# A gated unit at the DMA limit: all loads and stores on one queue, in the order store i, load i+2

## Chip, cores, metric

One core of one Trainium2 chip. The metric is device time in microseconds (us), the median of several executions. The experiments were spread over five chips; each was timed beside the kernel before, whose median lay between 933.28 and 933.66 us on all of them.

## The reference

```python
x = randn(8192, 8192) as float32          # 268 MB read
a, b = np.split(x, 2, axis=-1)
return a * (1 / (1 + np.exp(-b)))         # 8192 x 4096 float32, 134 MB written
```

## The kernel before

The input is cut into 32 tiles of 256 rows. A tile is 128 partitions by 64 KB (two rows side by side, each `a | b`), its output 128 partitions by 32 KB. There are two input slots and two output slots. ScalarE takes the sigmoid of `b` in place, VectorE multiplies. Loads are issued by the sync sequencer, stores by the scalar sequencer. Tiles 0 and 31 are worked in four chunks; tile 31 is also stored in four.

```python
R = 2; SLOTS = 2
x_t = x.rearrange("(n p r) m -> n p (r m)", p=P, r=R)
out_t = out.rearrange("(n p r) m -> n p (r m)", p=P, r=R)
xs = [pool.tile([P, R * n_cols], fp32, ...) for k in range(SLOTS)]
os = [pool.tile([P, R * half], fp32, ...) for k in range(SLOTS)]
...
for i in range(n_tiles):
    load = nc.sync.dma_start(out=xs[i % SLOTS], in_=x_t[i])     # waits for multiply i-2
    ...
    def store(cols):
        ins = nc.scalar.dma_start(out=out_t[i, :, cols], in_=os[i % SLOTS][:, cols])
    for k, (r, c) in enumerate(parts):      # one part; four in tiles 0 and 31
        sig = nc.scalar.activation(out=b, in_=b, func=SIG)
        mul = nc.vector.tensor_mul(out=packed[:, r, c], in0=rows[:, r, 0, c], in1=b)
        ...   # `implied(...)` drops waits that follow from others; in odd tiles
        ...   # the sigmoid, not the multiply, waits for the output slot
        if i == n_tiles - 1 and k > 0:
            store(chunks[k - 1])
    store(chunks[-1] if i == n_tiles - 1 else slice(0, R * half))
```

## Time and profile before

| | before |
|---|---|
| time | 933.28 us (933.08 to 933.77, 3 runs) |
| span of the profiled run | 931.7 us |
| bytes | 402.67 MB, 432 GB/s over the span |
| ScalarE, VectorE busy | 24%, 30% |
| DMA busy | 90% or more in each of 40 slices |

The table says that the 16 DMA engines never rest, so the kernel stands at the transfer limit; its lines are shown in the prediction. Beside the profile's views I use the trace's packet records: the start, length, size and queue of each packet that a DMA engine moved. Joining each packet to the one that starts where it ends gives 16 chains, one for each engine. The list of packets that one queue has on one engine is called its ring below.

### The profile page before, as it was taken

How to read it: one execution, taken by the hardware profiler on the slowest of the kernel's cores; microseconds unless marked ns; L12 is line 12 of the kernel's file. 1: busy time of each engine (PE TensorE's matmuls, PEld its weight loads, DVE VectorE, ACT ScalarE, POOL GpSimd, SP SyncE). 2: the span in 40 equal slices, each digit the busy share in tenths (PEclk: the TensorE clock that was granted, in tenths of full speed). 3: DMA queues.
4: the chain of work that ended last, by engine and by line, in shares of the span. 5: the costliest groups of instructions: out<-in, count | busy, mean ns of one | idle time of the engine just before them, and what ended most of it. 6: DMA issues, size and time to landing. Idle time of an engine off the chain costs nothing.

```text
span 931.7 us, 247 instructions
## 1 busy us (share of the span) xinstructions
DVE 278.7 (30%) x38; ACT 227.1 (24%) x39; POOL 0.2 (0%) x4
## 2 busy tenths in 40 slices
DVE  0333213333133331233312333123331233312333
ACT  1323330233311333113331133311333113332033
POOL 0000000000000000000000000000000000000000
DMA  9999999999999999999999999999999999999999
GB/s 405 428 450 428 422 456 405 450 428 428 450 418 438 428 436 442 428 428 450 447 408 428 442 459 428 413 460 411 450 428 425 453 408 447 428 428 450 425 430 405
DMA packets 9649, 402.67 MB, mean 432 GB/s; under 512 B 1072, under 2 KB 1072, under 8 KB 1072
## 3 DMA queue, kind: packets, MB, share of 16 engines
q1 hardware_dynamic: 4608, 268.44, 66.6%
q10 hardware_dynamic: 5040, 134.22, 33.4%
q14 instruction: 1, 0.01, 0.0%
HBM read 268.44 MB, written 134.22 MB: 432 GB/s over the span
## 4 chain that ended last, share of the span: by engine, by line
DMA 73%; DVE 15%; ACT 12%; issue 0%; ACTq 0%
DMA x_sb<-in_x_dram 73%; DVE o_sb L69 15%; ACT x_sb L68 12%; ACTq L62 0%; ACTq L68 0%
## 5 line engine op out<-in xcount | busy, mean ns | idle before, releaser
L69 DVE TENSOR_TENSOR o_sb<-x_sb 128x8192 f32<-128x8192 f32 (+1 forms) x38 | 278.7, 7344 | 647.1 <-ACT x_sb L68 647.1
L68 ACT ACTIVATE x_sb<-x_sb 128x8192 f32<-128x8192 f32 (+1 forms) x38 | 225.8, 5952 | 695.6 <-DMA x_sb<-in_x_dram 694.4
L68 ACT ACT_TABLE_LOAD x1 | 1.3, 1283 | 0.8 <-PEq L188 0.8
L188 POOL MEMSET const-bfloat16-1.0<- 128x1 bf16 x1 | 0.1, 102 | 0.0
L188 POOL MEMSET const-uint8-127<- 128x1 uint8 x1 | 0.1, 102 | 0.0
L188 POOL MEMSET const-float32-0.0<- 128x1 f32 x1 | 0.1, 99 | 0.2 <-issue 0.2
L188 POOL MEMSET const-float32-1.0<- 128x1 f32 x1 | 0.1, 99 | 0.0
## 6 DMA issues: line engine op xcount, KB each, us to landing
out_dram<-o_sb ACTq DMA_DIRECT2D x31, 4096.0 KB, 34.7
out_dram<-o_sb ACTq DMA_DIRECT2D x4, 1024.0 KB, 5.6
x_sb<-in_x_dram SPq DMA_DIRECT2D x32, 42.2
```

The costliest lines, as they stand in the source:

```text
L68: sig = nc.scalar.activation(out=b, in_=b, func=SIG)
L69: mul = nc.vector.tensor_mul(out=packed[:, r, c], in0=rows[:, r, 0, c], in1=b)
L188: nc = _bacc.Bacc("TRN2", target_bir_lowering=False, num_devices=1)
```

## The change

The intent: loads and stores share one first-in-first-out queue, so that each load runs at the full rate, each store follows in its turn, and the scalar sequencer is left to compute. The final tile's small stores stay on the scalar queue, so that they need not stand behind the last whole store.

```diff
+    def load(i, queue):
+        ins = queue(out=xs[i % SLOTS], in_=x_t[i])
+        ...
+    for i in range(SLOTS):
+        load(i, nc.sync.dma_start)
     for i in range(n_tiles):
-        load = nc.sync.dma_start(out=xs[i % SLOTS], in_=x_t[i])
         ...
-            by_sigmoid = i % 2 == 1 and len(parts) == 1
-            implied(mul, *(s for s in old["stores"] if by_sigmoid or s not in freed))
-            if by_sigmoid: ...                  # slot's wait on the sigmoid
+            implied(mul, *(s for s in old["stores"] if s not in freed))
             if i == n_tiles - 1 and k > 0:
-                store(chunks[k - 1])
-        store(chunks[-1] if i == n_tiles - 1 else slice(0, R * half))
+                store(chunks[k - 1], nc.scalar.dma_start)
+        if i == n_tiles - 1:
+            store(chunks[-1], nc.scalar.dma_start)
+        else:
+            store(slice(0, R * half), nc.sync.dma_start)
+        if i + SLOTS < n_tiles:
+            load(i + SLOTS, nc.sync.dma_start)
```

More of the change, by code (lines that the diff above doesn't have):

```diff
@@ L42, in _tiles @@
     last_stores = [[] for _ in range(SLOTS)]
+    loads = []
+    def load(i, queue):
+        old = gone[i % SLOTS]
+        ins = queue(out=xs[i % SLOTS], in_=x_t[i])
+        implied(ins, *old["loads"], *old["sigs"])
+        loads.append(ins)
+    for i in range(SLOTS):
+        load(i, nc.sync.dma_start)
     for i in range(n_tiles):
@@ L46, in _tiles @@
         now = {k: [] for k in old}
+        now["loads"].append(loads[i])
         rows = xs[i % SLOTS].rearrange("p (r h m) -> p r h m", r=R, h=2)
         packed = os[i % SLOTS].rearrange("p (r m) -> p r m", r=R)
-        load = nc.sync.dma_start(out=xs[i % SLOTS], in_=x_t[i])
-        implied(load, *old["loads"], *old["sigs"])
-        now["loads"].append(load)
         if 0 < i < n_tiles - 1:
@@ L60, in _tiles, with store @@
             ]
-        def store(cols):
-            ins = nc.scalar.dma_start(out=out_t[i, :, cols], in_=os[i % SLOTS][:, cols])
+        def store(cols, queue):
+            ins = queue(out=out_t[i, :, cols], in_=os[i % SLOTS][:, cols])
             now["stores"].append(ins)
@@ L71, in _tiles @@
             implied(mul, *old["muls"], *old["loads"], *now["loads"])
-            by_sigmoid = i % 2 == 1 and len(parts) == 1
-            implied(mul, *(s for s in old["stores"] if by_sigmoid or s not in freed))
-            if by_sigmoid:
-                for s in freed:
-                    tc.add_manual_dep(sig.ins, s.ins.name, DEP, reason="frees the output slot")
+            implied(mul, *(s for s in old["stores"] if s not in freed))
             tc.keep_in_program_order(sig)
```

## The prediction

> **What bounds the kernel now.** I read the page's engine shares first, then its DMA lines, then a table of stretches, then the waits and the timeline. The page, with the row of busy tenths for DMA in 40 slices:
>
> ```profile
> span 931.7 us, 247 instructions
> DVE 278.7 (30%) x38; ACT 227.1 (24%) x39; POOL 0.2 (0%) x4
> ...
> DMA  9999999999999999999999999999999999999999
> ...
> q1 hardware_dynamic: 4608, 268.44, 66.6%
> q10 hardware_dynamic: 5040, 134.22, 33.4%
> ...
> HBM read 268.44 MB, written 134.22 MB: 432 GB/s over the span
> ```
>
> The two compute engines are idle 70% and more; DMA is at 90% or above in every slice. Queue q1 (loads, sync) and q10 (stores, scalar) together fill 66.6 + 33.4 = 100% of 16 engines' span, in the ratio of their bytes (2 to 1). Is there a hole hidden in the rounding? The table of stretches (start:end, length, busy DVE, ACT, POOL, PE clock, DMA share, GB/s) says no for the body:
>
> ```profile
> 60.58:118.66 58.08, 17.39 (x2) 14.06 (x2) 0.00 (x0) 1.00 1.00 433
> 118.66:873.00 754.34, 226.00 (x26) 182.81 (x26) 0.00 (x0) 1.00 1.00 434
> ```
>
> DMA share 1.00 over two tiles and over 26 tiles. The trace's own packet records go further. Packets start in rounds of 16 (one per DMA engine), and each round starts when the previous ends. A round of load packets (64 KB each) lasts 2.415 us, so a load (8 rounds) takes 19.32 us; a round of store packets (32 KB) lasts 1.211 us, a 4 MB store 9.69 us; a final 1 MB store, eight rounds of 8 KB packets at 0.308 us, takes 2.47 us. Sum: 32 x 19.32 + 31 x 9.69 + 4 x 2.47 = 928.5 us. Add 1.0 us before the first packet and 1.55 us by which 32 early load packets run longer than their usual 2.418 us (start of the kernel, and 36 us, at the first store): 931.1 us. The last packet ends at 931.37. So all but 0.3 us of the run is packets back to back, and the bound is **bytes through 16 DMA engines**. The chain of waits (73% load, 15% multiply, 12% sigmoid) is misleading here: it follows the slot loop, whose "load" share includes 19 us in which that load stands behind others.
>
> **What the waits say about the slot loop.** Waits (total us, times, longest), then issues (count, KB, us to landing):
>
> ```profile
> ACT x_sb L68 <- DMA x_sb<-in_x_dram: 694.4, 32, 22.3
> SPq L50 <- DVE o_sb L69: 859.9, 30, 31.7
> out_dram<-o_sb ACTq DMA_DIRECT2D x31, 4096.0 KB, 34.7
> out_dram<-o_sb ACTq DMA_DIRECT2D x4, 1024.0 KB, 5.6
> x_sb<-in_x_dram SPq DMA_DIRECT2D x32, 42.2
> ```
>
> The sync sequencer does nothing but wait for the multiply of tile i, then issues load i+2. That load lands 42.2 us later although its data needs 19.3 us: it queues behind load i+1 and shares with stores. A store needs 9.7 us and lands in 34.7, because it shares with loads.
>
> **What the Trainium skill says.** "DMA: Bandwidth & Descriptors", section "Queues, rings and completion order": each DMA engine takes turns between the queue rows it has work for, a packet at a time, and consumes one row's descriptors in ring order. The trace agrees with the turns: after 40 us the rounds alternate, one of loads, one of stores. Same page, section "Issuing engines are not separate DMA queues": all issuers' transfers "run on the same 16 DMA engines and interleave", and a second issuer saves only sequencer time. The trace agrees: the two queues' shares add up to 100%, and the issue that moves costs 0.36 us. Same page, "Where 436 GB/s comes from": a ceiling of 435.2 GB/s for a core; the body here runs at 434, so by this too nothing is left in the rate.
>
> **The change, part by part.**
>
> *Stores move to the sync queue.* 31 issues of 0.36 us leave the scalar sequencer (11 us in total, where ACT waits 694 us for loads: worth nothing) and join the sync sequencer, which waits 860 us of 932. Store i and load i+2 wait for the same multiply, so neither holds back the other; the load is issued about 0.35 us later than now.
>
> *Sharing becomes first in, first out.* The ring order becomes L0 L1 S0 L2 S1 L3 ... The bytes and packet sizes are the same, so the work stays 928.5 us; the question is only whether the ring ever runs dry. Follow tile i, whose load lands at t. Sigmoid 7.03 us, multiply 8.69 us and handoffs take it to t + 15.8: then S(i) and L(i+2) are issued. At about t - 1.6 (in the first load, the last packet ends at 21.58 at the latest and ACT starts at 21.95; at the last, 913.1 and 914.7; I take the longer) the ring turned to S(i-1) and L(i+1), 29.0 us of work, so it runs dry at t + 27.4. The new work arrives **11.6 us** before that. The first two loads fill the ring to 1.0 + 0.7 + 2 x 19.32 = 40.3, and the first multiply is over at
>
> ```profile
> 21.95 7.31 ACT L68 ACTIVATE x_sb<-x_sb 128x2048 f32<-128x2048 f32 x4 [19.89 <-DMA x_sb<-in_x_dram]
> 23.89 8.90 DVE L69 TENSOR_TENSOR o_sb<-x_sb 128x2048 f32<-128x2048 f32 x4 [23.89 <-ACT x_sb L68]
> 32.82 0.38 ACTq L62 DMA_DIRECT2D out_dram<-o_sb  x1
> ```
>
> 32.82 us, 7.5 us early. Landing times follow: a store 11.6 + 9.7 + 1.6 = 23 us (now 34.7), a load 11.6 + 9.7 + 19.3 + 1.6 = 42.2 us (as now). Output slots are free long before they are wanted, so taking the slot's wait from sigmoid to multiply costs nothing. Effect on the end: 0.
>
> *The tail.* Now S30 shares with L31, and L31's data is in at 913.1. In the new order S30 stands behind L31, so L31 is in one store's part earlier: 931.4 - (9.69 + 4 x 2.47) = 911.8, landing at 913.4. The scalar queue's stores came 4.3, 6.5, 8.9 and 11.1 us after the landing in the old tail:
>
> ```profile
> 914.71 3.71 ACT L68 ACTIVATE x_sb<-x_sb 128x2048 f32<-128x2048 f32 x2 [21.75 <-DMA x_sb<-in_x_dram]
> ...
> 918.98 0.34 ACTq L62 DMA_DIRECT2D out_dram<-o_sb  x1
> 921.18 0.34 ACTq L62 DMA_DIRECT2D out_dram<-o_sb  x1
> 923.63 2.54 ACTq L62 DMA_DIRECT2D out_dram<-o_sb  x2
> ```
>
> So issues at about 917.7, 919.9, 922.3, 924.5. S30 keeps the engines busy until 921.5 alone; the four small stores need 2.47 us each after it, starting at the latest at 921.5, 924.0, 926.4, 928.9. Each is issued about 4 us ahead, and the only doubt is how soon its packets follow. The tail should stay filled: 0, perhaps +2 us (below).
>
> Sum: 0 + 0 + 0 to 2; expected 0.1. From 933.28, **933.4 us**.
>
> **Rivals.**
>
> 1. *A bubble where a load follows a store in one ring.* Now the other queue could cover such a bubble. Against: load 0 to load 1 is a boundary inside one ring with the other empty, and the rounds start at 16.18, 18.59, 21.01, 23.42: no bubble at 21.01. The final stores also follow each other in one ring at 0.308 us a round without a step. No boundary between a store and a load in one ring can be seen before. 62 such boundaries at 0.05 us would make 936.4; slower by over 2% needs 18.7 us, 0.30 us each, about an eighth of a load packet. I give 3%.
>
> 2. *The scalar queue's first use.* The first store of all was issued at 32.82 and its first packets started at 38.81, 6 us later, with one load round stretched by 0.87 us. That queue's first use now falls in the tail. With 6 us of delay the first small store would start at 923.7 instead of 921.5: +2.2 us, 935.5. For it: it was seen. Against: in those 6 us two 2.4 us load rounds were already under way; behind 1.21 us store rounds the wait is shorter.
>
> 3. *A gain, from fewer turns between reads and writes or a shorter tail.* Loads alone (1 to 35 us) run at 2.415 us a round and stores alone (914 to 921) at 1.211, the same as mixed, so turns cost nothing to be saved; and no idle time is left to fill. At best the stretched first packets go: -1.5 us, 931.8. Faster by 2% would need over 450 GB/s. 1%.
>
> **Range and chances.** Down: 1.5 us of start-up plus a little noise (three runs span 0.7 us). Up: rival 2, or a small rival 1. Range 931.8 to 936.4; faster 0.01, same 0.96, slower 0.03.
>
> **What would show it right or wrong.** Right: DMA share 1.00 at 434 GB/s in the body, q1 holding nearly all bytes, stores landing in 23 us, loads in 42 us, sync still mostly waiting for multiplies, the second load landing near 42 us (now 44.8). Rival 1: share under 1.00 in the body and load rounds that step by more than 2.415 us at a change of direction. Rival 2: a hole around 921 to 924 us only. Wrong altogether: loads landing later than 43 us with ACT waiting over 22 us a tile, which would mean a cost of a single ring that no row here shows.

## The result

The changed kernel took **938.15 us** (936.89 to 940.78, 4 runs) against 933.24 (933.08 to 933.77, 4 runs). The ratio is **1.0055**, 95% interval 1.004 to 1.007. A ratio is the mean time of one kernel's runs over that of the other's of the same rounds, so not quite the ratio of the medians. Executions over 1.5% slower than the fastest of the same kernel are left out of the means. The loss is clear of noise, and the time lies above the predicted range of 931.8 to 936.4.

The page of the changed kernel:

```profile
span 935.5 us, 235 instructions
DVE 278.8 (30%) x38; ACT 227.0 (24%) x39; POOL 0.2 (0%) x4
...
DMA  9999999999999999999999999999999999999998
...
q1 hardware_dynamic: 9072, 398.46, 98.7%
q10 hardware_dynamic: 576, 4.19, 1.1%
```

Nearly all bytes are now on q1. The DMA row looks full; only the last slice shows something, 8 for 9. The stretches over two tiles and 26 tiles (columns as in the prediction: DMA share and GB/s last):

```profile
58.58:116.98 58.40, 17.38 (x2) 14.06 (x2) 0.00 (x0) 1.00 1.01 434
116.98:874.19 757.21, 226.01 (x26) 182.76 (x26) 0.00 (x0) 1.00 1.00 433
```

The same two tiles took 58.08 us before and take 58.40 now, the same 26 tiles 754.34 and 757.21: most of the 3.8 us of span is lost in the body, at a DMA share of 1.00. The waits and issues:

```profile
ACT x_sb L76 <- DMA x_sb<-in_x_dram: 695.8, 32, 22.6
SPq L70 <- DVE o_sb L77: 874.3, 31, 31.6
out_dram<-o_sb SPq DMA_DIRECT2D x31, 4096.0 KB, 22.9
x_sb<-in_x_dram SPq DMA_DIRECT2D x32, 41.8
```

A store lands 22.9 us after its issue (23 predicted), a load 41.8 (42.2 predicted). So the queue works as worked out. The tail, on the timeline:

```profile
916.02 3.71 ACT L76 ACTIVATE x_sb<-x_sb 128x2048 f32<-128x2048 f32 x2 [21.95 <-DMA x_sb<-in_x_dram]
...
920.29 0.38 ACTq L70 DMA_DIRECT2D out_dram<-o_sb  x1
922.49 0.91 ACTq L70 DMA_DIRECT2D out_dram<-o_sb  x1
```

The last load was to land at 913.4; the sigmoid that waits for it starts at 916.02, 2.6 us later. Where do these come from, if the engines were never idle?

**The packet records show it.** An engine's packet of load is 2.418 us long in the rule. The last load packet ahead of a store is longer than that ("stretched") on 1 to 16 engines, by 0.05 to 0.6 us (up to 1.1 in a second record, taken later), and what an engine loses so it keeps: it runs behind the others from then on. How far the slowest is behind the fastest is called the lag. When each engine came to its first packet of the store of tile k:

```
                   fastest engine (us)         slowest engine behind it (us)
store of tile      0      7      16     30      0     4     7     12    16    30
changed kernel   41.35  244.74 505.76 911.76   0.76  1.16  2.45  3.13  3.90  3.90
a second record  41.41  244.6  505.6  911.6    0.62  3.21  3.96  5.04  5.64  5.72
before: the 16 semaphore writes that close a load lie 0.6 us apart, in every tile
```

The fastest engine keeps 29.00 us a tile and reaches the last store at 911.76; the prediction had 911.8. The slowest, 3.90 us behind, still has that store (9.69 us) and four small ones (9.88 us) before it: 911.76 + 3.90 + 9.69 + 9.88 = 935.2. The last packet of the record ends at 935.15. The second record gives 936.9 by the same sum, and ends at 936.8. So the loss in these records is **the lag of the slowest of 16 engines**. A transfer is not done until its slowest engine is (the last packet of load 31 ends at 915.66, and its sigmoid starts at 916.02), while the busy share, a mean over engines that are all busy, shows none of this.

### The profile page after: what moved, and what is told of

Its sections match the earlier page's. It is cut to its first block, busy times and chain, and to the rows that moved or that the text cites. A ratio compares the mean times of both kernels' runs of the same rounds, so it can differ in the third digit from the quotient of the medians.

```text
span 935.5 us, 235 instructions
## 1 busy us (share of the span) xinstructions
DVE 278.8 (30%) x38; ACT 227.0 (24%) x39; POOL 0.2 (0%) x4
## 2 busy tenths in 40 slices
DMA packets 9650, 402.67 MB, mean 430 GB/s; under 512 B 1072, under 2 KB 1072, under 8 KB 1072
## 4 chain that ended last, share of the span: by engine, by line
DMA 72%; DVE 15%; ACT 12%; SPq 1%; issue 0%; ACTq 0%
DMA x_sb<-in_x_dram 72%; DVE o_sb L77 15%; ACT x_sb L76 12%; SPq L70 1%; ACTq L70 0%
## 6 DMA issues: line engine op xcount, KB each, us to landing
out_dram<-o_sb SPq DMA_DIRECT2D x31, 4096.0 KB, 22.9
x_sb<-in_x_dram SPq DMA_DIRECT2D x32, 41.8
```

## The experiments

Three rivals at the start: the change of direction inside one ring (A), the moved wait and later issue (B), the first use of the scalar queue in the tail (D). That the first record was a one-off (C) is met by a second one. A loss of 0.5% counts as seen because its interval lies above 1. Each kernel has one packet record, but the changed kernel two.

### The changed kernel once more

No edit.

> The changed kernel unaltered, for a second packet record. In the first one the fastest DMA engine kept exactly 29.00 us a tile, but other engines had their last load packet ahead of a store stretched, by 0.05 to 0.6 us, at tiles 0 to 16 and hardly later, and fell up to 3.9 us behind the fastest. Theory A (a change from load to store inside one ring costs the engines that already lag): the same picture, some engines 3 to 5 us behind at the end, time 936.5 to 941. Theory C (a one-off of that run): lag under 1 us, time under 935.

938.47 us, ratio 1.0049 (1.0034 to 1.0064). Lag 5.7 us; load packets stretched after the first store by 21 us in all, summed over engines (25 in the first record), and hardly after tile 17. The picture repeats; which engines lag and by how much differs, and with it the time.

### Stores back on the scalar queue

```diff
-            store(slice(0, R * half), nc.sync.dma_start)
+            store(slice(0, R * half), nc.scalar.dma_start)
```

> The changed kernel with the 31 whole stores back on the scalar queue; the new program order and the wait moved from sigmoid to multiply stay. Theory A: the single ring is the cause, so 933.2 us, engines within 1 us of each other at the end. Rival B (the moved wait or the later load issue costs something): 936 to 938 us.

933.34 us, ratio 0.9995 (0.9978 to 1.0012); lag 1.3 us. All else of the change stays in this kernel, so B is refuted: the 5 us come from putting the stores on the loads' queue. Nor is it the step from a load packet to a store packet as such: with two rings each engine takes it for every one of its 248 store packets, and after the first store the load packets of this run are stretched by only 1.0 us in all, summed over engines.

### Final stores on sync as well

```diff
-                store(chunks[k - 1], nc.scalar.dma_start)
+                store(chunks[k - 1], nc.sync.dma_start)
...
-            store(chunks[-1], nc.scalar.dma_start)
+            store(chunks[-1], nc.sync.dma_start)
```

(The closing code then takes the last store of the sync queue.)

> The changed kernel with the final tile's four stores on the sync queue too. In its record eight engines had the first small packet of the scalar queue stretched by 0.8 to 1.1 us at 921.6, but those were not the engines that ended last. Theory A (lag of the slow engines sets the end): 937 to 938.5, at most 1 us less than the changed kernel. Rival D (the first use of the scalar queue in the tail costs the time): 934 or less.

938.65 us, ratio 1.0051: no gain, so D is refuted. Lag 4.5 us; the sum of above gives 911.45 + 4.52 + 19.57 = 935.5, and the last packet ends at 935.5.

### Loads on scalar, stores on sync

```diff
-            load(i + SLOTS, nc.sync.dma_start)
+            load(i + SLOTS, nc.scalar.dma_start)
```

> The changed kernel with loads 2 to 31 on the scalar queue and the stores left on sync: two rings again, with the queues' roles exchanged. If mixing directions in one ring is the cause, 933 to 933.8 us and a lag under 1.5 us. If stores on the sync queue are the cause, 938.

933.51 us, ratio 0.9999; lag about 1 us. Which queue carries what does not matter, as long as they are two. This run has a lesson in reading waits. Stores now take 49.2 us to land, and the multiply waits for them:

```profile
ACT x_sb L76 <- DMA x_sb<-in_x_dram: 690.2, 32, 22.6
DVE o_sb L77 <- DMA out_dram<-o_sb: 374.6, 19, 20.3
```

A new wait of 374.6 us in all costs nothing, because the DMA engines always have other work queued.

### Load i+2 ahead of store i

```diff
-            store(slice(0, R * half), nc.sync.dma_start)
-        if i + SLOTS < n_tiles: load(i + SLOTS, nc.sync.dma_start)
+            if i + SLOTS < n_tiles: load(i + SLOTS, nc.sync.dma_start)
+            store(slice(0, R * half), nc.sync.dma_start)
```

> The changed kernel with load i+2 issued ahead of store i: still one ring and 31 changes from load to store, but each store is in the ring about 31 us before its turn instead of 12. If the stretching is a matter of late descriptors: gone, 933.5. If it is the change of direction in one ring: as the changed kernel, 937 to 940, lag 3.5 to 6 us.

938.89 us, ratio 1.0059; lag 4.9 us. The stores stand in the ring long before their turn, and the loss is the same. It is not a matter of issuing late.

### Halves: twice the changes, or twice the transfers

Three kernels cut each load and each store in two by row. In the first, the ring order is store, load, store, load; in the second, store, store, load, load; in the third, stores are on scalar.

```diff
-            store(slice(0, R * half), nc.sync.dma_start)
+            for h in range(2):
+                store(slice(h * half, (h + 1) * half), nc.sync.dma_start)   # third: nc.scalar
+                load(i + SLOTS, nc.sync.dma_start, (h,))                    # first kernel only
```

First:

> Loads and stores of the changed kernel cut into halves by row, in ring order store, load, store, load: twice the changes from load to store in one ring, packets of half the size. Packets of half the size alone cost perhaps 0.5% (an 8 KB packet takes 0.309 us, a quarter of a 32 KB one 0.303), so about 4 us. Theory A with a fixed cost for each change: the lag of the slowest engine doubles, to 7 us, time 945. Theory A with a lag that ends by itself once engines are some us apart: lag about 4 us again, time 941.

Second:

> Halves again, but in ring order store, store, load, load: 31 changes from load to store as in the changed kernel, twice the transfers, packets of half the size. In the three whole-size records the stretching of load packets ended at tile 17, in the store-load-store-load run at tile 9, both after 17 to 18 changes and some 36 transfers. If what counts is changes of direction (or the lag they have built up): stretched packets only at the change to a store, until about tile 17, lag 3.5 to 5 us, time 939 to 941. If what counts is transfers in the ring: they end at about tile 9.

Third:

> The same halves with the stores on the scalar queue: prices the smaller packets alone. From the store-load-store-load run, whose packets add up to 3.5 us more for an engine on average than the changed kernel's: 935.5 to 937, lag under 1.5 us.

Measured: 939.05, 940.4 and 936.29 us; lag 3.5, 4.6 and 1.2 us. The third prices smaller packets at 2.7 us (ratio 1.0029). Against it, one ring costs 2.8 and 4.1 us. (The first had been forecast at 941 or 945; the smaller packets had been taken for 4 us.) In the first, stretching died out after tile 9, some 18 changes, with the lag at 3.3; in the second it faded about tile 17, after 17 changes but twice the transfers. By these two records it is changes from load to store that count, not transfers; and doubling them does not double the loss. The lag grows over some 17 changes and then stands, here and in the records of the changed kernel.

### Engines put out of step on purpose

```diff
+    for q in (0, 32):      # 8 partitions each: carried out by half of the engines
+        nc.sync.dma_start(out=os[1][q : q + 32 : 4, :], in_=x_t[1][q : q + 32 : 4, : R * half])
```

Once with one ring, once with stores on scalar.

> The changed kernel with two dummy loads of 8 partitions by 32 KB behind load 1, which only half of the engines carry out: these start 2.4 us behind the rest before the first store. If the lag limits itself (engines stretch packets while they cross from load to store together), the stretching after the first store falls well below the 16 to 25 us, summed over engines, of the three records, and the time is about 938 to 940 with a lag no larger than before. If it adds to whatever lag there is: lag 6.5 to 8 us, time 940.5 to 942.

> The two dummy loads of the skewed kernel with the stores on the scalar queue. Half the engines start 2.4 us behind. If the lag alone were what costs (engines out of step), 940 or more; if it costs only together with one ring for both directions: 933.3 plus the 2.4 us of the dummy loads, 935.5 to 936.5, and no stretched packets beyond the first store.

One ring: 944.66 us, ratio 1.0119. Two rings: 936.0 us, 1.0029. The second is as expected: lag stands at 4.5 us, and two rings are not hurt by it. The first missed both of its forecasts. The lag ended at 4.6 us, no larger than before; but now all engines, leading ones too, had packets stretched by about 1 us at some changes (such as those near 127, 215, 303, 420, 567 and 829 us) and by almost nothing at others: 119 us after the first store, summed over engines, against 25 and 21 before. My theory that being apart protects engines fell with this run: with two groups a packet apart, packets were stretched more, not less.

### Pauses in the stores, in two rings

In one ring an engine runs no store while it runs a load, so writing pauses, for 18.6 us at most and 15.4 in late tiles of the first record. Is the pause the cause, rather than the ring? Loads in halves give load and store packets one size, 32 KB; taking turns, a whole store is then done before the next comes.

```diff
-        ins = queue(out=xs[i % SLOTS], in_=x_t[i])
+        for h in range(2):
+            ins = queue(out=xs[i % SLOTS][:, cols_h], in_=x_t[i][:, cols_h])
...                                     # whole stores, on nc.scalar.dma_start
```

> Two rings with pauses in the writing: loads in halves (32 KB packets) on sync, whole stores (32 KB packets) on scalar. Taking turns packet by packet, a store now needs 19.4 us of each 29.0 us tile, so every tile has some 9.7 us without a store and then starts storing anew, as in one ring, but in another ring. If the start of storing after a pause is what stretches the loads in flight: stretched packets at many tiles, lag of several us, time over 936. If it needs both directions in one ring: lag under 1.5 us and 933 to 936 (the smaller load packets may cost up to 2 us of the 2.7 us that halves of both cost).

**958.51 us**, ratio 1.0242 (1.0198 to 1.0286): the worst of all with whole work done, and with two rings. (At 2% this is "unclear", because the interval reaches down to 1.0198; that it is slower is beyond doubt. The forecast said only "over 936".) One stretch of 754 us, first of the kernel with stores back on scalar, then of this one:

```profile
118.00:872.00 754.00, 225.84 (x27) 182.76 (x26) 0.00 (x0) 1.00 1.00 434
```

```profile
118.00:872.00 754.00, 225.85 (x26) 175.73 (x25) 0.00 (x0) 1.00 1.00 421
```

The share is 1.00 in both; the rate falls from 434 to 421 GB/s. The engines are busy, with packets that take longer. Stores pair up here, with 19.5 to 20.1 us between pairs in which none runs. Each time storing starts again, load packets are stretched, mostly by 12 to 20 us summed over 16 engines, about 1 us each. Over the run this and smaller stretches make 19.7 us an engine; some 4 of them are on store packets. With the stores in halves too (the third kernel of halves) the pauses are gone after the first tiles and so is the loss: 936.29.

### One ring with the pauses filled, and two rings with pauses put in

Two kernels cut each whole store into two eighths and a rest. In one the eighths go on scalar, where their 4 KB packets take turns with load packets and keep a store in flight; in the other all three are on sync.

```diff
-            store(slice(0, R * half), nc.sync.dma_start)
+            e = R * half // 8
+            store(slice(0, e), nc.scalar.dma_start)        # second kernel: nc.sync
+            store(slice(e, 2 * e), nc.scalar.dma_start)    # second kernel: nc.sync
+            store(slice(2 * e, R * half), nc.sync.dma_start)
```

> The changed kernel with each whole store cut in three: two eighths (4 KB packets) on the scalar queue, six eighths behind the load on sync. The small packets take turns with the load packets, one each, so a store is in flight through most of the loads and no long pause in writing is left, while the sync ring still changes from load to store 31 times. If the start of storing after a pause is the cause: the loads' stretching after the first store falls to under 6 us summed over engines, lag under 2 us. If mixing directions in one ring is enough: 15 to 25 us and a lag of 3.5 to 6 us, as in the changed kernel.

> The same three pieces, all on sync: same packets, pauses in writing as long as in the changed kernel. Both theories: stretching of 15 to 25 us summed over engines and a lag of 3.5 to 6 us; its time against that of the run with the small pieces on scalar shows what the pauses cost, 2 to 5 us.

The third keeps two rings and leaves five stores out (a wrong result):

```diff
-        else:
-            store(slice(0, R * half), nc.sync.dma_start)
+        elif i not in (5, 10, 15, 20, 25):
+            store(slice(0, R * half), nc.scalar.dma_start)
```

> Two rings (stores on scalar), with the stores of tiles 5, 10, 15, 20 and 25 left out: a wrong result on purpose. Each gap leaves over 15 us without a store, in a kernel without one ring for both. If the start after a pause is the cause: five further events of about 1 us on all 16 engines, 80 us summed over engines, time 933.3 - 5 x 9.69 + 5 = 890. If the one ring is needed: no stretching but the first store's, 885.

Measured: 940.11 us with the eighths on scalar, 949.62 with all on sync. Their packets are the same; the mean engine's stretching is 2.4 us in the first and 8.7 in the second. But the first did not do what the pause theory asked. Its pauses are 6.5 us at most after the first store, yet its lag grew to 4.6 us, with 13 us of stretching summed over tiles 1 to 17 (forecast: under 6 if the pause is the cause, 15 to 25 if one ring is enough). So **in one ring the pause is not needed**. The second lost more than either theory said, and its stretching went on to the end. Its pauses shrink from 18.4 to 9.2 us; a load alone takes 19.3, so by the last store the slowest engine is some 10 us behind.

Leaving stores out gave four pauses of 20.6 to 20.8 us and one of 28.5 (start and end of each from the packet records). The last three restarts stretched load packets by 25 to 26 us summed over engines, the first by 1.7, the second by 3.5 at once and 7.8 more in the next 10 us. So a pause in two rings is able to cost 1.5 us on every engine, but not at every restart. The profiled execution took 893.5 us (890 expected if the pause is the cause, 885 if one ring is needed), the three others 910.7 to 915.1. I have no record of those three, and their 20 us more stay unexplained; this run counts for its packet record only.

### How much of a store must stand behind the load?

The first part of each store goes on scalar, the rest on sync behind the load: four eighths, then six.

```diff
-            store(slice(0, R * half), nc.sync.dma_start)
+            e = R * half // 8 * 4                       # second kernel: * 6
+            store(slice(0, e), nc.scalar.dma_start)
+            store(slice(e, R * half), nc.sync.dma_start)
```

> The changed kernel with the first half of each whole store (16 KB packets) on scalar and the second half behind the load on sync. The sync ring still changes from load to store 31 times, and writing already runs at 16 KB to every 64 KB loaded when it does. If the size of the jump in writing is what stretches loads: lag under 2.5 us, stretching after the first store under 6 us summed over engines. If any store behind a load in the ring does it: lag 3.5 to 6 us. Packets of half the size add about 1.5 us: 935.5 against 940.

> The same with six eighths (24 KB packets) on scalar and two eighths (8 KB) on sync. If the size of the jump counts: as two rings, lag under 1.5 us, 935 us. If any store behind a load in the ring does it: lag 3.5 to 6 us, 940.

939.6 and 939.4 us (ratios 1.0066 and 1.0064), lag 5.9 and 6.4 us at the last loads. The smaller packets account for some 2 us of these times. A quarter of a store behind a load costs about as much as a whole one; the size of the jump in writing is refuted. (Both kernels still have pauses of 12 to 14 us, so they alone would not exclude the pause; the run with the pauses filled does.)

### Together

From the packet records and the times; "full rate" is all packets at their usual length, "stretched" what they took beyond it, both for the mean engine.

| kernel | rings | full rate | stretched | lag | last packet ends | time |
|---|---|---|---|---|---|---|
| before | two | 929.7 | 1.5 | 0.6 | 931.4 | 933.3 |
| stores back on scalar | two | 929.7 | 1.5 | 1.3 | 931.9 | 933.3 |
| queues swapped | two | 929.7 | 1.7 | 1 | 931.9 | 933.5 |
| changed kernel | one | 929.7 | 3.5 | 3.9 | 935.2 | 938.2 |
| the same, second record | one | 929.7 | 3.0 | 5.7 | 936.8 | 938.5 |
| final stores on sync | one | 929.7 | 2.9 | 4.5 | 935.5 | 938.7 |
| load ahead of store | one | 929.7 | 3.0 | 4.9 | 936.0 | 938.9 |
| quarter of each store on sync | mixed | 931.7 | 3.4 | 6.4 | 937.9 | 939.4 |
| eighths on scalar | mixed | 933.9 | 2.4 | 4.6 | 937.9 | 940.1 |
| eighths on sync | one | 933.9 | 8.7 | about 10, by its pauses | 946.9 | 949.6 |
| pauses in the stores | two | 931.8 | 19.7 | to 4.7 | 959.2 | 958.5 |

"Time" is the median of four; "last packet ends" is of the one profiled execution, so the two need not move together. 1.5 us of stretching, at the start and at the first store, is common to most.

## Why the prediction was wrong

**Right.** The kernel is bound by bytes through 16 engines. The ring never runs dry: store and load landings were forecast at 23 and 42.2 us and measured at 22.9 and 41.8, and the fastest engine reached the last store at 911.76 (911.8). The sequencers' issues, the moved wait and the slots cost nothing (933.34 with all of these and two rings). The tail as such cost nothing either.

**Rival 2 did not happen.** The first packets of the first small store began 1.1 us after its issue at 920.29, not 6. Six engines had that first packet stretched by 0.8 to 1.1 us (the forecast under "Final stores on sync" says eight), but these were leading engines with time to spare, and moving the stores to sync gained nothing.

**Rival 3 rightly got nothing.** There was no gain to find. Its "over 450 GB/s" for a gain of 2% is too high: 402.67 MB in a span 2% shorter (931.7 x 0.98 = 913 us) are 441 GB/s. Another slip changed nothing either: a load stands 13 us behind the one before it (issued at 60.58, the other landed by 73.65), not 19.

**The step that failed** is "so the work stays 928.5 us; the question is only whether the ring ever runs dry", with its "Effect on the end: 0". It took 16 engines for one stream. They do not move as one: in place of 0, the slowest engine gained 3.3 us of lag (0.6 before, 3.9 in the first record; 5.1 in the second), and that lag is the loss. Rival 1 had named the place, a change of direction within one ring, but mis-sized it, for two reasons. It leaned on load after load and store after store in one ring, neither of which is the change that matters; and it spread a small bubble evenly over 62 changes and all engines. Measured: only changes from load to store, of which there are 31; only in the first 17 or so; 0.05 to 0.6 us on 1 to 16 engines at a time (up to 1.1 in the second record). The 25 us of stretching are 1.6 us for the mean engine, less than the 3.1 us of that rival; but the slowest gathered 3.3, and 933.28 + 3.3 = 936.6 is already past the range's end of 936.4. The sign it named, a share under 1.00, could not come, because a stretched packet counts as busy; its other sign, longer load packets at a change, did.

**What stays open.** Shown: a store behind a load in one ring is enough for the lag, whatever its size, order of issue or the queue of the tail; two rings without long pauses do not have it; long pauses in storing can cost in two rings as well. Not shown: what inside an engine holds the last load packet, why only some engines, why the lag stops growing after some 17 changes in most one-ring kernels, and why it did not stop, at twice the loss and more, with each store in three pieces in one ring (949.62 us). That engines spread apart protect each other was tried and failed.

## What to carry to other kernels

At the DMA limit, ask not only whether the queues stay full but whether all 16 engines stay in step: a transfer ends with its slowest engine, and a full busy row hides a lag. Keep loads and stores on two queues, and size the packets so that some store is nearly always in flight; here 64 KB load packets against 32 KB store packets, the same ratio as the bytes, did that at 434 GB/s, while equal packets made pauses and fell to 421. And a new wait, even one of 375 us, costs nothing as long as the engines have other work queued.

## What the Trainium skill lacked or had wrong

- "DMA: Bandwidth & Descriptors", section "Issuing engines are not separate DMA queues", says that issuing from several engines only saves sequencer time. Here putting stores on the loads' queue cost 5 us (938.15 against 933.24) and undoing just that brought it back (933.34), although the sequencers had time to spare. For bandwidth the two queues share, the page agrees with the trace; for keeping engines in step, it is not the whole story.
- The same page, section "Queues, rings and completion order", has nothing on how far the engines of one transfer come apart when loads and stores share a ring, and I found no figure for it elsewhere: 0.6 to 1.3 us with two rings (without pauses or skew), 3.5 to 6.4 us in most kernels with loads and stores in one.
- No page that I read tells that starting to store after a pause of some 20 us can stretch the load packets in flight, here by about 1 us on each engine, 25 us in a run (958.51 against 933.32), of which 2 are the price of smaller packets.
- "Queues, rings and completion order" gives the turns by packet, which the trace confirms, but draws no consequence for packet sizes, and I found none elsewhere: 64 KB against 32 KB kept a store in flight nearly all the time, 32 KB against 32 KB did not.
